# Issuing the first 8 MB load as eight loads of 16 partitions each, ahead of the preamble barrier

## The chip, the cores and the metric

The kernel runs on one core of a Trainium2 chip. The metric is device time in microseconds (us) of one execution. Ratios are the mean time of one kernel's runs over the mean time of the kernel before in the same rounds, so they are not quite the ratio of the medians that are quoted beside them.

HBM is the memory that holds `x` and `out` (the page of the kernel before: 134.22 MB read, 67.11 MB written), SBUF the memory that holds the tiles, which the kernel addresses as 128 partitions (rows). ACT, DVE and SP are three of the core's engines; the traces list their instruction queues as ACTq, DVEq and SPq. ACT computes the silu, DVE the product, SP only issues stores. The 16 DMA engines move the data. A packet is one record of a DMA engine in the trace, here the bytes of one partition.

## The reference

```python
x = randn(32, 512, 2048).astype(float32)
x1, x2 = x[..., :1024], x[..., 1024:]
out = (x1 * (1 / (1 + exp(-x1)))) * x2        # silu(x1) * x2, float32, (32, 512, 1024)
```

The kernel reads 134 MB, writes 67 MB, and does two elementwise operations per output element. There is no matrix multiplication.

## The kernel before

The 16,384 rows are cut into 16 tiles of 1,024 rows. Partition `p` of a tile holds 8 neighbouring rows, 65,536 contiguous bytes both in HBM and in SBUF. There are two input buffers and two output buffers. Loads are issued on ACT's queue and stores on SP's. The first load is moved ahead of the barrier at the head of the program.

```python
K = 8; KC = 2
in_pool  = ctx.enter_context(tc.tile_pool(name="in_pool",  bufs=2))
out_pool = ctx.enter_context(tc.tile_pool(name="out_pool", bufs=2))
...
def load(i):
    xt = in_pool.tile([P, K, in_cols], dt, name="xt")          # 128 x 65,536 B
    nc.scalar.dma_start(out=xt[:, :plan[i][1], :], in_=view(x_flat, i))
    loaded[i] = xt

load(0)
load(1)
for i in range(n_tiles):
    ...
    for c in range(0, k, KC):                                  # four chunks of 128 x 2048
        nc.scalar.activation(out=ot[:, c:ce, :], in_=xt[:, c:ce, :half], func=Silu)
        nc.vector.tensor_mul(out=ot[:, c:ce, :], in0=ot[:, c:ce, :], in1=xt[:, c:ce, half:])
        # the last tile stores each chunk, the others the whole tile
    if not last:
        nc.sync.dma_start(out=ov, in_=ot[:, :k, :])
    if i + 2 < n_tiles:
        load(i + 2)
```

## Time and profile before

| | before |
|---|---|
| time, median of 4 runs | 471.0 us (470.53 to 471.09) |
| profiled span | 468.9 us |
| share of the 16 DMA engines' time: loads + stores | 66.4% + 33.2% |
| DVE busy, ACT busy | 30%, 25% |
| one load packet (65,536 B, one partition) | 2.418 us, 27.1 GB/s |
| first activation starts | 21.88 us |

These are lines of the profile page of the kernel before: the span in 40 slices (busy tenths of DMA, and what the engines moved), the queues (q10 is ACT's queue with the loads, q1 is SP's with the stores), and the chain of waits that ended last.

```profile
...
DMA  9899999999999998999999999999999989999998
GB/s 431 375 447 403 447 447 447 403 419 431 447 447 403 447 492 363 442 492 391 458 403 439 456 447 403 409 442 447 447 403 444 467 386 447 442 419 481 400 409 354
...
q10 hardware_dynamic: 2304, 134.22, 66.4%
q1 hardware_dynamic: 2736, 67.11, 33.2%
...
DMA 80%; DVE 15%; ACT 3%; DVEq 0%; issue 0%
...
```

The reader should see that DMA is at nine tenths or nearly so in every slice, that the two queues together fill 99.6% of the engines' time, and that the compute engines are mostly idle. The kernel is one unbroken stream of DMA packets. With 99.6% filled I take it that the time changes only if the engines lose time.

The timeline of the opening (start, duration, engine, line, operation, and in brackets the idle time before it) shows the first two loads, which have the engines to themselves until the first store packet starts, 37.7 us after the first load packet in the records:

```profile
...
0.13 1.13 ACTq L74 DMA_DIRECT2D xt<-in_x_dram  x2
...
1.29 1.28 ACT L87 ACT_TABLE_LOAD   x1 [1.29 <-PEq L117]
21.88 7.31 ACT L87 ACTIVATE ot<-xt 128x2048 f32<-128x2048 f32 x4 [19.31 <-DMA xt<-in_x_dram]
...
44.54 1.91 ACT L87 ACTIVATE ot<-xt 128x2048 f32<-128x2048 f32 x1 [15.36 <-DMA xt<-in_x_dram]
```

The first load feeds the activations at 21.88 us, and the second, 22.7 us later, those at 44.54 us.

Besides these views the trace has a record of every DMA packet. I sort the load packets by start time in rows of 16, one per engine, and quote start (us after the first of them) + duration. Before, the first three rows have these ranges:

```
packets of the kernel before, first load (8 rows of 16)
row 1   starts 0.00 to 0.70    durations 2.47 to 3.44
row 2   starts 3.09 to 3.46    durations 2.418 to 2.434
row 3   starts 5.51 to 5.88    durations 2.418 to 2.420
```

### The profile page before, as it was taken

The numbers are of one execution on the slowest core, as the hardware profiler recorded it, in microseconds if no ns is written. First come the engines' busy times: TensorE is split into PE (matmuls) and PEld (weight loads), VectorE is DVE, ScalarE is ACT, GpSimd is POOL, SyncE is SP. The second block draws the span as 40 slices with busy tenths as digits, with TensorE's granted clock in tenths as the row PEclk, the third lists the DMA queues.
The fourth block names the chain that finished last, engine by engine and source line by source line (L and its number), as shares of the span: only waits on it lengthen the run. The fifth ranks groups of instructions, "written<-read, shape, count | busy, mean of one in ns | idle before, by whom it ended". The sixth has DMA issues, their size and how long they took to land.

```text
span 468.9 us, 269 instructions
## 1 busy us (share of the span) xinstructions
DVE 142.3 (30%) x64; ACT 118.2 (25%) x65; POOL 0.2 (0%) x4
## 2 busy tenths in 40 slices
DVE  0070705106061160601507025070250702407034
ACT  1142406023060330603206032060420604106051
POOL 0000000000000000000000000000000000000000
DMA  9899999999999998999999999999999989999998
GB/s 431 375 447 403 447 447 447 403 419 431 447 447 403 447 492 363 442 492 391 458 403 439 456 447 403 409 442 447 447 403 444 467 386 447 442 419 481 400 409 354
DMA packets 5042, 201.35 MB, mean 429 GB/s; under 512 B 560, under 2 KB 560, under 8 KB 560
## 3 DMA queue, kind: packets, MB, share of 16 engines
q10 hardware_dynamic: 2304, 134.22, 66.4%
q1 hardware_dynamic: 2736, 67.11, 33.2%
q14 instruction: 2, 0.02, 0.0%
HBM read 134.22 MB, written 67.11 MB: 429 GB/s over the span
## 4 chain that ended last, share of the span: by engine, by line
DMA 80%; DVE 15%; ACT 3%; DVEq 0%; issue 0%
DMA xt<-in_x_dram 80%; DVE ot L92 15%; ACT ot L87 3%; DVEq L128 0%
## 5 line engine op out<-in xcount | busy, mean ns | idle before, releaser
L92 DVE TENSOR_TENSOR ot<-ot,xt 128x2048 f32<-128x2048 f32 x64 | 142.3, 2286 | 319.5 <-ACT ot L87 319.5
L87 ACT ACTIVATE ot<-xt 128x2048 f32<-128x2048 f32 x64 | 116.9, 1897 | 338.8 <-DMA xt<-in_x_dram 338.8
L87 ACT ACT_TABLE_LOAD x1 | 1.3, 1283 | 1.3 <-PEq L117 1.3
L117 POOL MEMSET const-uint8-127<- 128x1 uint8 x1 | 0.1, 102 | 0.0
L117 POOL MEMSET const-bfloat16-1.0<- 128x1 bf16 x1 | 0.1, 101 | 0.0
L117 POOL MEMSET const-float32-0.0<- 128x1 f32 x1 | 0.1, 98 | 0.2 <-issue 0.2
L117 POOL MEMSET const-float32-1.0<- 128x1 f32 x1 | 0.1, 98 | 0.0
## 6 DMA issues: line engine op xcount, KB each, us to landing
out_dram<-ot SPq DMA_DIRECT2D x15, 4096.0 KB, 39.8
out_dram<-ot SPq DMA_DIRECT2D x4, 1024.0 KB, 5.7
xt<-in_x_dram ACTq DMA_DIRECT2D x16, 47.1
```

The source lines that it names most:

```text
L87: nc.scalar.activation(out=ot[:, c:ce, :], in_=xt[:, c:ce, :half], func=mybir.ActivationFunctionType.Silu,)
L92: nc.vector.tensor_mul(out=ot[:, c:ce, :], in0=ot[:, c:ce, :], in1=xt[:, c:ce, half:],)
L117: nc = _bacc.Bacc("TRN2", target_bir_lowering=False, num_devices=1)
```

## The change

The intent is to get the first bytes moving sooner with smaller DMAs; whether that works is what the run has to show. The first load of 8.4 MB is issued as eight loads of 1.05 MB, each for 16 neighbouring partitions, all ahead of the barrier. The bytes, the packets (one 65,536 B row per partition) and all later loads stay.

```diff
-def issue_ahead_of_the_first_barrier(nc):
+def issue_ahead_of_the_first_barrier(nc, count):
     head, body = nc.main_func.blocks[:2]
-    load = next(ins for ins in body.instructions if type(ins).__name__ == "InstDMACopy")
+    loads = [ins for ins in body.instructions if type(ins).__name__ == "InstDMACopy"][:count]
... (moves all of `loads` instead of `load`)
+    FIRST = [16] * 8
...
-        nc.scalar.dma_start(out=xt[:, :plan[i][1], :], in_=view(x_flat, i))
+        p = 0
+        for np_ in FIRST if i == 0 else [P]:
+            nc.scalar.dma_start(out=xt[p:p + np_], in_=view(x_flat, i)[p:p + np_])
+            p += np_
```

More of the change, by code (lines that the diff above doesn't have):

```diff
@@ L6 @@
 from concourse._compat import with_exitstack
-def issue_ahead_of_the_first_barrier(nc):
+def issue_ahead_of_the_first_barrier(nc, count):
     head, body = nc.main_func.blocks[:2]
-    load = next(ins for ins in body.instructions if type(ins).__name__ == "InstDMACopy")
+    loads = [ins for ins in body.instructions if type(ins).__name__ == "InstDMACopy"][:count]
     at = next(
         j for j, ins in enumerate(head.instructions)
-        if ins.engine == load.engine and type(ins).__name__ == "InstDrain"
+        if ins.engine == loads[0].engine and type(ins).__name__ == "InstDrain"
     )
-    body.instructions = [ins for ins in body.instructions if ins.name != load.name]
-    head.instructions = head.instructions[:at] + [load] + head.instructions[at:]
+    names = {ins.name for ins in loads}
+    body.instructions = [ins for ins in body.instructions if ins.name not in names]
+    head.instructions = head.instructions[:at] + loads + head.instructions[at:]
 @with_exitstack
@@ L63, in view @@
         return flat[row0:row0 + P * k].rearrange("(p k) d -> p k d", k=k)
-    nc.at_finalize(issue_ahead_of_the_first_barrier)
+    nc.at_finalize(lambda nc: issue_ahead_of_the_first_barrier(nc, len(FIRST)))
     ctx.enter_context(tc.manual_schedule())
```

## The prediction

> **What bounds the kernel now.** The DMA engines. In the queue table the loads take 66.4% and the stores 33.2% of the 16 engines' time, 99.6% together, at 429 GB/s over the 468.9 us span; DVE is busy 30%, ACT 25%. The chain that ended last is 80% loads. The first two loads have the engines alone: the first activation starts at 21.88 us, the fifth at 44.54 us (timeline). The trace's DMA records hold 128 packets of 65,536 B per load, one per partition, 8 per engine, each 2.418 us (27.1 GB/s): 19.3 us. So the kernel is one unbroken stream, and only lost engine time can move it.
>
> **What the change does.** Bytes, packets (one 65,536 B row per partition) and all later loads stay. The first load becomes eight of 16 partitions: each engine gets one row per piece.
>
> 1. Issue. Seven more issues on ACT at about 0.35 us (the page's took 0.33 to 0.38) are 2.5 us, hidden behind queued transfers. In the records of before, the packet after a completion write starts 6 ns later: no bubble per piece.
> 2. Start. The stream starts about 1.1 us into the span; a smaller first DMA may gain some tenths.
> 3. Waits. As built, the second load waits for the first piece (semaphore reuse), and the activation table load for six pieces, so its 1.28 us falls after them. Both hide behind queued transfers.
> 4. Where the rows go. [...] I expect the first load to land at 65 to 78 us, not 21.9, and the second about 19 us later.
>
> **How much is critical.** All of point 4: during the first load nothing else can run, the queue behind it is held, and the stream has no slack. [...] I take 46.
>
> **Predicted time:** 517 us, range 486 to 530. Faster by over 2%: 0.01; within 2%: 0.14; slower by over 2%: 0.85.
>
> **What would show it.** First activation at 65 to 78 us; GB/s in the opening slices near 110 to 170 instead of 375 to 447, while the DMA busy share stays high (first-load packets of 5 to 10 us instead of 2.4); from the second load on the pace of before, shifted by a constant; the chain begins with a load piece of 65 to 78 us; equal byte counts.
>
> **What would make it wrong.** [...] packets stay at 2.4 us, the first activation comes at 22 to 24 us and the time within 1% of 471. [...]

Terms of this prediction are cut, and the places marked. Point 4 named a cause and worked out from it the loss with all engines in step, and a smaller one with engines that drift out of step; the 46 us was chosen between the two. No trace or run of this case shows that cause, so it is gone, and with it the arithmetic and the conditions under "What would make it wrong". What is left of the sum is 471 us before + 46 us lost = 517 us. Read the 46 us, the 65 to 78 us for the first load, the 110 to 170 GB/s and the packets of 5 to 10 us as forecasts whose derivation is not shown.

## The result, and the profile after

The changed kernel takes 524.99 us (median of 4 runs, 524.6 to 526.28) against 471.0 us: ratio 1.1153, 95% interval 1.1133 to 1.1174. It is 54 us slower.

The same lines of the page, for the kernel after:

```profile
...
DMA  9797799998999999999999999999999999999988
GB/s 160 80 160 80 85 160 476 401 481 388 453 401 441 441 441 421 426 436 481 401 441 421 421 481 436 406 441 406 476 401 441 471 398 413 441 438 473 441 386 346
...
q10 hardware_dynamic: 2416, 134.22, 69.9%
q1 hardware_dynamic: 2736, 67.11, 29.8%
...
DMA 65%; DVE 15%; another core or an unknown queue 14%; ACT 4%; DVEq 0%; issue 0%; ACTq 0%
...
```

In the first six slices the engines still count as busy, but they move 80 to 160 GB/s. From the seventh slice on the profile is that of before (346 to 481 GB/s, before 354 to 492). This is the line to learn from: a DMA engine that is held up looks busy (seven tenths or more at 80 to 160 GB/s), so a busy share has to be read beside the GB/s. The chain of waits now has 14% that the view gives to "another core or an unknown queue"; in order of time three of its four pieces (64.6 us) lie between 12.35 and 77.10 us, where the first load's pieces are landing one after another, and the fourth (9.1 us) is the wait for the second load, from 89.7 to 98.8 us. So the chain does not begin with one load piece of 65 to 78 us, as was forecast, but with a piece of 11.85 us and these three.

The timeline of the opening after:

```profile
...
0.12 12.23 ACTq L78 DMA_DIRECT2D xt<-in_x_dram  x9
...
77.19 1.28 ACT L92 ACT_TABLE_LOAD   x1 [77.19 <-DMA xt<-in_x_dram]
78.48 7.31 ACT L92 ACTIVATE ot<-xt 128x2048 f32<-128x2048 f32 x4
...
98.83 7.31 ACT L92 ACTIVATE ot<-xt 128x2048 f32<-128x2048 f32 x4 [13.04 <-DMA xt<-in_x_dram]
...
```

The first activations start at 78.48 us, 56.6 us later than before, and the second tile's at 98.83 us, 54.3 us later. The total is 54.0 us longer, so everything after the second tile is only shifted. The table load (L92 ACT_TABLE_LOAD, 1.28 us) now waits for the pieces and delays the first tile, but by the second tile the DMA stream behind it has absorbed that.

This is engine activity by stretch of time in the kernel after (stretch, length, busy time of each engine, granted clock, DMA share, GB/s; a packet's bytes are booked at its start, so short stretches are rough: the one from 1 to 2 us reads 1049 GB/s):

```profile
...
20.00:30.00 10.00, 0.00 (x0) 0.00 (x0) 0.00 (x0) 1.00 0.94 105
30.00:40.00 10.00, 0.00 (x0) 0.00 (x0) 0.00 (x0) 1.00 0.94 105
40.00:50.00 10.00, 0.00 (x0) 0.00 (x0) 0.00 (x0) 1.00 0.94 105
100.00:150.00 50.00, 17.79 (x8) 13.45 (x8) 0.00 (x0) 1.00 0.99 430
...
```

In each of the 10 us stretches exactly 16 packets start, 1.05 MB. The packet records say it directly:

```
packets of the kernel after, first load (one row = one piece)
row 1   starts  0.00 to  0.64   durations 7.36 to 9.20
row 2   starts  7.39 to  9.27   durations 9.35 to 9.36
row 3   starts 16.74 to 18.62   durations 9.34 to 9.35
...
row 8   starts 63.45 to 65.32   durations 9.34
row 9   starts 72.79 to 74.66   durations 3.12 to 4.51    (first packets of the second load)
row 10  starts 77.30 to 77.81   durations 2.42 to 2.43
```

The durations of the first load's 128 packets add up to 19.99 us per engine before and 73.93 us after, a difference of 53.9 us. The other 1,920 load packets add up to 291.1 and 291.3 us. The whole loss of 54.0 us is these 128 packets. What remained to be shown was what makes them slow, and why the drift between engines on which I counted gave nothing back.

### The profile page after: what moved, and what is told of

Read it like the earlier page. It is cut to its first block, busy times and chain, and to the rows that moved or that the text cites. A ratio compares the mean times of both kernels' runs of the same rounds, so it can differ in the third digit from the quotient of the medians.

```text
span 523.3 us, 285 instructions
## 1 busy us (share of the span) xinstructions
DVE 142.4 (27%) x64; ACT 118.2 (23%) x65; POOL 0.2 (0%) x4
## 4 chain that ended last, share of the span: by engine, by line
DMA 65%; DVE 15%; another core or an unknown queue 14%; ACT 4%; DVEq 0%; issue 0%; ACTq 0%
DMA xt<-in_x_dram 65%; DVE ot L97 15%; ACT ot L92 3%; DVEq L133 0%; ACT L92 0%; ACTq L78 0%; ACTq L92 0%
## 5 line engine op out<-in xcount | busy, mean ns | idle before, releaser
L92 ACT ACTIVATE ot<-xt 128x2048 f32<-128x2048 f32 x64 | 116.9, 1897 | 317.3 <-DMA xt<-in_x_dram 317.3
```

## The experiments

Theory P says that the packets of a piece are slow because of the SBUF partitions to which they go together: 16 neighbouring ones at a time are bad, all 128 are not. I had a reason for it, on which the forecasts of 4.7 us for wider or spread pieces rested. No trace or run shows that reason; P's forecasts stand as forecasts, and the runs show which of them held. The rivals are these: N, the number of DMAs, their waits and completion writes; S, small pieces are slow whichever partitions they take; H, reading 16 neighbouring rows of HBM at once is slow; B, only packets within the same group of four neighbouring partitions collide; and the position ahead of the barrier.

All twelve experiments are in this table; the packet column is the median of the load packets concerned.

| experiment | first load | us | ratio | packet |
|---|---|---|---|---|
| before | one DMA, 128 partitions | 471.0 | 1 | 2.418 us |
| after | 8 x 16 neighbouring partitions | 524.99 | 1.1153 | 9.34 us |
| e1_rows | 8 x all 128 partitions, one row each | 471.84 | 1.0013 | 0.309 us for 8,192 B |
| e4_both_strided | 8 x 16 partitions, every eighth | 491.15 | 1.0422 | 5.11 us |
| e5_source_strided | 8 x 16 neighbouring, HBM rows every eighth | 524.45 | 1.1129 | 9.29 us |
| e6_dest_strided | 8 x 16, every eighth, HBM rows neighbouring | 491.46 | 1.0429 | 5.11 us |
| e2_32 | 4 x 32 | 490.91 | 1.0417 | 5.12 us |
| e3_64 | 2 x 64 | 491.42 | 1.0428 | 5.12 us |
| e7_two_queues | as after, half the pieces on SP | 524.82 | 1.1137 | 9.28 us |
| e8_third_load | third load in eight, not the first | 523.84 | 1.1116 | 8.5 us |
| e9_after_barrier | as after, seven pieces behind the barrier | 525.56 | 1.1164 | 9.37 us |
| e10_skew | 2 + 7 x 16 + 14 | 533.6 | 1.1335 | 9.37 us |
| e11_store | loads as before; first store in 8 x 16 | 480.66 | 1.0211 | store packets 1.21 to 2.81 us |
| e12_one_port | one DMA, behind 4 small loads to partitions 0..3 and 32..35 | 490.53 | 1.0417 | 8.5 to 9.25 us for 24 packets, then 2.42 us |

### Eight loads that span all partitions

```diff
-                nc.scalar.dma_start(out=xt[p:p + np_], in_=view(x_flat, i)[p:p + np_])
+                nc.scalar.dma_start(out=xt[:, r:r + 1, :], in_=v[:, r:r + 1, :])   # r = 0..7
```

> Eight first loads ahead of the barrier as in the change, 1 MB each, but each spans all 128 partitions (one row of 8192 B per partition). Theory P [...]: [...] nothing is lost; the first load's packets run at full rate, first activation at 22 to 24 us, time 469 to 473 us. Rival N (eight DMAs, their completion writes, the waits and the late table load cost it): like the changed kernel, about 525 us.

It took 471.84 us; the interval of the ratio, 0.9996 to 1.0029, contains 1. The timeline of this run:

```profile
...
0.12 4.14 ACTq L79 DMA_DIRECT2D xt<-in_x_dram  x8
...
5.36 1.28 ACT L94 ACT_TABLE_LOAD   x1 [5.36 <-DMA xt<-in_x_dram]
7.45 1.91 ACT L94 ACTIVATE ot<-xt 128x2048 f32<-128x2048 f32 x1 [0.81 <-DMA xt<-in_x_dram]
...
12.49 1.91 ACT L94 ACTIVATE ot<-xt 128x2048 f32<-128x2048 f32 x1 [3.13 <-DMA xt<-in_x_dram]
...
22.43 1.91 ACT L94 ACTIVATE ot<-xt 128x2048 f32<-128x2048 f32 x1 [3.05 <-DMA xt<-in_x_dram]
...
```

The number of first loads, their place ahead of the barrier and the wait of the next load for the first piece are as in the changed kernel, the table load again waits for loads (it starts at 5.36 us, before at 1.29), and nothing is lost. Rival N falls. The expectation was wrong in a detail: the first activation came at 7.45 us and not at 22 to 24, because the first chunk needs only the first two of these loads. That head start of 14 us bought nothing (ratio 1.0013), as was to be expected of a kernel whose DMA stream fills 99.6% of the engines' time.

### Which side matters: HBM rows or SBUF partitions

```diff
 for j in range(8):
-    dma_start(out=xt[16*j:16*j+16], in_=v[16*j:16*j+16])   # the change
+    dma_start(out=xt[j:P:8],        in_=v[j:P:8])          # e4_both_strided
+    dma_start(out=xt[16*j:16*j+16], in_=v[j:P:8])          # e5_source_strided (first tile wrong on purpose)
+    dma_start(out=xt[j:P:8],        in_=v[16*j:16*j+16])   # e6_dest_strided   (first tile wrong on purpose)
```

> Eight pieces of 16 partitions, but piece j takes partitions j, j+8, ... and the rows that belong to them. Theory P: [...] packets near 4.7 us instead of 9.34, first activation near 39 to 41 us, time about 489 us. Rival S (16-partition pieces are slow by themselves, whichever partitions): 525 us. Rival H (16 neighbouring rows of HBM read at once are slow): 471 us.

> Wrong result on purpose in the first tile: piece j writes partitions 16j to 16j+15 as the change does, but reads rows j, j+8, ... of HBM. Theory P: destination unchanged, so 9.3 us packets, first activation near 78 us, 525 us. Rival H (neighbouring HBM rows): 471 us, or 489 if the stride is only half as good.

> Wrong result on purpose in the first tile: piece j reads the 16 neighbouring rows that the change reads, but writes partitions j, j+8, ... Theory P: [...] packets near 4.7 us, first activation near 40 us, about 489 us. Rival H (source) and rival S (piece size): 525 us, as the change.

With the change this is a two-by-two table, and the time follows the SBUF partitions alone: neighbouring partitions 524.99 and 524.45 us, every eighth partition 491.15 and 491.46 us, whatever the HBM rows. H falls. S falls too, because pieces of the same size lose 20 us or 54 us depending on which partitions they take. So does B: every eighth partition puts each of the 16 packets of a piece in a group of four of its own, which should have given 2.4 us. The packet time was 5.11 us and not the 4.7 expected (half of 9.34); theory P was right in direction and about 8% low in size. The waits of ACT on the first load in e5, and below it in e6 (waited for, us in total, times, longest), differ accordingly:

```profile
...
ACT L94 <- DMA xt<-in_x_dram: 76.8, 1, 76.8
...
```

```profile
...
ACT L94 <- DMA xt<-in_x_dram: 43.6, 1, 43.6
...
```

### Twice and four times as many partitions per piece

```diff
-    FIRST = [16] * 8
+    FIRST = [32] * 4       # e2_32
+    FIRST = [64] * 2       # e3_64
```

> Four pieces of 32 partitions. Theory P: [...] packets near 4.7 us, first activation near 39 us, about 489 us. A cost per DMA (rival N) would give half of the change's loss for half the pieces, about 498 us, with packets of 2.4 us.

> Two pieces of 64 partitions. Theory P [...]: [...] packets near 4.7 us, about 489 us, no better than 32 partitions. Rival B (what collides is the group of four neighbouring partitions[...]): [...] packets of 2.4 us and 471 us. Rival N (cost per DMA): about 484 us with 2.4 us packets.

32 and 64 partitions cost the same, 490.91 and 491.42 us, with packets of 5.12 us in both. B expected 2.4 us for 64 partitions, if each engine then works in a group of four of its own; the records do not name engines, so here the run is only against B, and it is e4 and e6 that rule it out. A cost per DMA would have made two pieces cheaper than four. So 64 neighbouring partitions per piece were no better than 32, as theory P forecast; why that is so the runs do not show.

### Place and queue

```diff
-    nc.at_finalize(lambda nc: issue_ahead_of_the_first_barrier(nc, len(FIRST)))
+    nc.at_finalize(lambda nc: issue_ahead_of_the_first_barrier(nc, 1))              # e9_after_barrier, e8_third_load
-        for np_ in FIRST if i == 0 else [P]:
+        for np_ in FIRST if i == 2 else [P]:                                        # e8_third_load
-            nc.scalar.dma_start(...)
+            (nc.sync if i == 0 and p >= 64 else nc.scalar).dma_start(...)           # e7_two_queues (4 moved ahead)
```

> The change's eight pieces, but only the first is issued ahead of the preamble barrier, the other seven after it. Theory P: the first piece alone lasts 9 us, far longer than the later issue, so nothing changes: about 525 us, first activation near 78 us. If issuing all eight ahead of the barrier had a share in the loss, the time falls below 520 us.

> The first load whole; the third load (the one beside the first store) in eight pieces of 16 partitions, so neither the barrier nor the start of the program plays a part. Theory P: the same loss, [...]: about 525 us, 9.3 us packets in that load. If the cost belonged to the start (issue ahead of the barrier, late table load), about 471 us. If the stores of the other queue fill the gaps, somewhere between, 480 to 510 us.

> The change's eight pieces, but the upper four (partitions 64 to 127[...]) are issued on SP. Theory P, with each engine working on one packet at a time and all engines in step, gives no gain: packets of 9.3 us, about 525 us. If the two queues let the engines get out of step, [...] packets fall toward 4.7 us and the time to 490 to 510 us.

Behind the barrier (525.56 us) or in the third load (523.84 us) the loss is the same, so neither the barrier nor the start of the program is its cause. In e8 the load runs beside the stores of the other queue, and they do not fill the gap: from 70 to 130 us of that run the engines moved 156 to 193 GB/s (windows of 10 to 20 us). Here is the timeline of that run around the third load:

```profile
...
33.01 23.66 ACTq L78 DMA_DIRECT2D xt<-in_x_dram  x8
56.71 7.31 ACT L92 ACTIVATE ot<-xt 128x2048 f32<-128x2048 f32 x4 [27.27 <-DMA xt<-in_x_dram]
...
135.36 7.31 ACT L92 ACTIVATE ot<-xt 128x2048 f32<-128x2048 f32 x4 [71.34 <-DMA xt<-in_x_dram]
...
```

The third tile starts at 135.36 us, 102 us after its load was issued; the typical load of the kernel before lands in 47 us. The load's packets took 8.45 us (median), somewhat less than the 9.3 expected. The store packets that started meanwhile went from 1.21 to 1.68 us (median): they were slowed too, but by far less than the loads. Over two queues (e7) the packets of ACT and SP alternate row by row in the records and still take 9.28 us each: no gain. As each row holds packets of one queue only, the engines stayed in step, and the run does not show what lower and upper partitions at the same time would give.

### Does a lead help, and whom does a narrow load slow?

In the records of the kernel after, one engine is 0.96 us ahead of all others when it enters the second piece, which goes to other partitions (16 to 31). If only packets of the same piece slowed each other, it should have gained. It kept 9.35 us per packet and the same lead to the end. Two runs asked why.

```diff
-    FIRST = [16] * 8
+    FIRST = [(126,128)] + [(16*j, 16*j+16) for j in range(7)] + [(112,126)]         # e10_skew
```

> Two rows (partitions 126 and 127) go first in a DMA of their own[...]; then seven pieces of 16 and one of 14. [...] If engines in step is what kept drift from helping, [...] some 32 of the 128 packets take about 5.1 us while the other 96 keep 9.3 us; [...] the time stays within 5 us of 525 us. If a lead does not help [...], all packets of the pieces stay near 9.3 us.

The second expectation held: no packet of the first load came near 5.1 us, and the median stayed at 9.37. All 16 packets of the first row took 6.9 to 8.7 us, and among them are the two of the leading DMA, which went to partitions 126 and 127, far from the 0 to 15 of the piece behind it. The time, 533.6 us, is 3.6 us above the band of 525 us plus or minus 5 that the first expectation gave; the second named none. If the two rows went to two engines (the records do not name engines), these had nine packets of the first load instead of eight, and the records do show two packets of 8.8 and 9.2 us that start after the eighth row and land last. The packets of the eighth row took 10.4 to 11.2 us; I did not settle why.

```diff
+    for b in range(2):
+        spare = out_pool.tile([P, K, half], dt, name="ot")      # free until the first store
+        for p in (0, 32):                                       # partitions 0..3, 32..35
+            nc.scalar.dma_start(out=spare[p:p+4]..., in_=view(x_flat, 0)[p:p+4, :4, :])   # 4 x 32,768 B
     load(0)                                                     # whole, as before
```

> The kernel before (first load whole) with four small loads put ahead of it on the same queue: each writes 4 rows of 32768 B, which nobody reads, into partitions 0..3 or 32..35 of a tile that is still free[...]. [...] Theory U [...]: the four engines take about 4.7 us per small packet, 18.7 us for four, while the other twelve run the first load at 2.4 us a packet (up to 3.5 for the very first). Theory C [...]: during those 18.7 us the other twelve get about 9.3 us a packet too, some 24 packets of 65536 B above 6 us. Either way the first activation comes near 40 us and the time rises by 8 to 20 us.

The question was whom a narrow load slows: by theory U only the engines that carry it, by theory C all 16, which then move at the pace of the slowest. (That partitions 0..3 and 32..35 belong together was my assumption; the run does not test it.)

These are the packet records of that run:

```
e12_one_port, starts from the first 65,536 B packet
small loads, 4 packets each:  starts -2.24 to -2.18  0.08 to 1.85  5.00 to 6.92  10.04 to 11.96
                              durations 2.32 to 4.03  4.92 to 5.09  5.03          5.03
first load, other 12 engines: starts 0.00 to 0.74, durations 8.55 to 8.94
                              starts 8.62 to 9.52, durations 8.52 to 9.25
then all 16 engines:          2.42 to 4.89, settling at 2.42
```

Exactly the 24 packets that theory C named took over 8.5 us, on the 12 engines that had no small load (the records do not name engines, but they show four small packets at a time and 12 large ones beside them). In the kernel before, where no small loads are ahead, the same load takes 2.47 to 3.44 us a packet in its first row and 2.42 to 2.43 in its second, so it is beside the small loads that all 12 were slowed. Theory U falls. The bytes added are 0.52 MB, 1.2 us at the rate of the stream (an estimate, 0.52 MB at 16 times 27.1 GB/s); the time rose by 19.7 us. The page shows it in the first slices:

```profile
...
GB/s 123 220 430 430 387 397 440 462 387 435 467 405 470 413 427 470 392 430 462 400 459 440 416 465 408 438 464 387 430 472 405 443 440 421 464 400 430 432 350 327
...
```

So here the four small loads set the pace of the loads on all 16 engines. The 12 engines moved 7.1 to 7.7 GB/s each (65,536 B in 8.52 to 9.25 us), nearly as little as the four that carried the small loads (32,768 B in 5.03 us, 6.5 GB/s). That would explain why the lead was worth nothing: an engine that is already in the next piece keeps the pace of those that are not (9.35 us). It fits row 9 of the kernel after, where the first packets of the second load, which goes to all 128 partitions, are still slowed, all 16: the one that starts first takes 4.51 us, the one that starts last, when the eighth piece is done, 3.12 us. One control is missing: the same four small loads aimed at partitions further apart were not run, so that small DMAs on four engines do this wherever they write is not excluded by e12 alone; the leading engine of the kernel after, which no small load was beside, speaks against it. What carries the coupling inside the chip no run here shows.

### The same shape in a store

```diff
-            nc.sync.dma_start(out=ov, in_=ot[:, :k, :])
+            for p in range(0, P if i == 0 else 1, 16): ...      # first store in eight pieces of 16 partitions
```

> The kernel before, with the first store (not a load) cut into eight pieces of 16 partitions. If reading SBUF [...] is held as writing is, the store's 32768 B packets take four times 1.213 us, about 4.9 us, and up to 29 us are lost: 490 to 500 us. If only writes into SBUF collide, packets stay at 1.2 us and the time at 471 us.

Neither expectation held. The store's packets took 1.21 to 2.81 us: 41 of the 128 took 1.21, the median was 1.61, and the 16 of the first piece, which ran at the same time, took 1.97 to 2.42. So in this setting reading SBUF from 16 neighbouring partitions at a time slowed the packets to at most 2.3 times their length, not to four times. The two runs, 478.27 and 483.06 us, are slower than before, but so far apart that the verdict is unclear (interval 1.009 to 1.0331). In the waits of the profiled one (478.27 us) the third tile waited 40.7 us for an output buffer. Most of that stands in place of waits for loads: all of ACT's waits of these two kinds add up to 344.2 us, against 338.8 before.

```profile
...
ACT ot L87 <- DMA xt<-in_x_dram: 296.8, 14, 24.0
ACT ot L87 <- DMA out_dram<-ot: 47.4, 2, 40.7
...
```

Before, ACT never waited for a store in this view. The store's packets start about 6 us apart per engine instead of 3.6, so it holds its buffer longer. The packet records show why it gets fewer turns. Each piece ends with a completion write of 4 B on every engine, and packets of the two queues alternate: in one such sequence (times in the span) a store packet starts at 43.16 us, a load packet at 44.51, the store's completion write of 9 ns at 46.92, another load packet at 46.93, and the next store packet at 49.35, each where the one before ends. There the tiny write took a whole turn of its queue, and two load packets (2 x 2.42 us) stood between store packets (1.21 us at least) instead of one. The packets themselves account for 5.2 us per engine of the 7.6 us by which the profiled span grew.

## Why the prediction was right

- **The bound** (an unbroken DMA stream that only lost engine time can move): right. The loss of 54.0 us is the 53.9 us by which 128 packets grew.
- **Point 1, issue and completion writes:** right. The same number of DMAs over all partitions costs nothing measurable (e1_rows, 1.0013).
- **Point 2, an earlier start:** no gain was seen; in both kernels the 16 first packets start between 1 and 2 us into the span.
- **Point 3, waits:** right in substance. The table load came after all eight pieces and not after six, moved to 77.19 us and made the first activation 1.28 us later; the second tile shows none of it.
- **Point 4, where the rows go:** right in its outcome. That the SBUF partitions decide was tested against the rivals by e4, e5, e6, e2 and e3; the cause that I gave for it no run here shows. A 16-partition DMA still ran on 16 engines: the records have the 16 packets of a piece at once. Eight rows in step took 8 x 9.34 = 74.7 us, against the forecast landing at 65 to 78.
- **Drift:** wrong, and it is the term of the sum that was mis-sized. The prediction took 46 us, less than the loss with all engines in step, because I assumed that engines that drift apart get part of it back. Here they did not: the leading engine of the kernel after kept 9.35 us a packet, and in e12_one_port the 12 engines without a small load were slowed (7.1 to 7.7 GB/s) nearly as much as the four that had one (6.5 GB/s). The loss, 54.0 us, was therefore close to that of eight rows in step (8 x 9.34 less 8 x 2.418 us is 55.4 us), and 517 us was 8 us too low, inside the range. For the same reason the first load landed at the upper end of 65 to 78 us (ACT's wait for it ended at 77.1), the table load then put the first activation at 78.48 us, just outside, and the opening GB/s (112 by packets, 1,048,576 B in 9.34 us) lay at the bottom of 110 to 170.

## What to carry to other kernels

Cut a load along the bytes inside the partitions and not along the partitions: eight loads of 128 x 8,192 B cost nothing at the start, where no other queue was busy, eight of 16 x 65,536 B cost 54 us, and 32 or 64 partitions per piece still cost 20 us. A narrow load was not only slow itself: in e12_one_port the loads on the other 12 DMA engines slowed from 2.42 to 8.5 to 9.25 us a packet while it ran, so 0.5 MB aimed at four partitions at a time cost 20 us. Beside a second busy queue a piece of a cut DMA also gave up a turn to its completion write: in e11_store two load packets of 2.42 us stood between store packets instead of one. When DMA reads as fully busy, look at the GB/s beside it and at the duration of a packet, for engines that were held up counted as busy here (0.94 at 105 GB/s).
